# A streaming encoder block on one core: the pool inputs' gates moved to slots 3 and 5 of the next pair, the output pair's forms made in three steps over two slots

## The chip, the core and the metric

The kernel runs on one core of a Trainium2 chip. Four engines do the work: PE multiplies matrices (its weight loads are shown apart as PEld), DVE does element-wise work on two operands, ACT does casts, copies and activation functions, POOL is nearly idle; SP issues transfers. Each engine works its own list of instructions in program order, and semaphores make one wait for another. The metric is the device time of one execution in microseconds (us). Three runs of the kernel before gave 1829.51, 1828.97 and 1829.35 us: median 1829.35.

## What is computed

One encoder block for 256 tokens of width 4096, in fp32. A mixer sub-layer projects the normalised tokens by one wide matrix and splits the result; one part feeds attention, another a multi-scale pooling whose output is gated. Both go through an output projection and onto the residual; a cross-attention sub-layer follows. The lines that the change concerns:

```python
q, k, v, gate_a, u_b, gate_b = jnp.split(h @ w_in, ...)
y_a = att * jax.nn.silu(gate_a)
y_b = multiscale_pool(u_b, w_pool, pool_scale) * jax.nn.silu(gate_b)   # 4 groups of 512 channels
y = jnp.concatenate([y_a, y_b], axis=-1) @ w_out
x = x + rmsnorm(y, g_post)
# multiscale_pool: trailing mean over 2, 4, 8 or 16 tokens, minus the token; then a 512 x 512 map; then a scale
# silu(g) = g * sigmoid(g) = 0.5 * g * (tanh(g / 2) + 1)
```

## The kernel before

**Weights as a stream.** All weights come as 648 chunks of 128 x 1024 ("subs"). PE works one sub per *slot*; the loop at line 1264 runs over slots. A fp32 product is made of three matmuls on rounded parts: a value is split into `wh`, its rounded value (ACT, line 201), and `wl`, what rounding left (DVE, line 202), and PE adds high x high, low x high and high x low (lines 324 to 326). A sub is split two or three slots ahead of the slot that uses it; there are four raw buffers and five pairs `wh`/`wl`, so the split engines can run ahead of PE by a few slots and no more.

**Pairs.** The first 520 subs are worked in 16 *pairs* of output strips: A and B for attention, then U 0 to 3 (the pool inputs with their gates), then O 0 to 3 (the output projection). A pair takes 32 slots; U 1 to 3 and O 0 take 34, since the two pool subs (512 x 512 map) of the U pair before stand in them. Most pairs save products on some of their 16 *quads* (two slots each) by working on sums of blocks: those quads are "fast" and need four splits, two of them of sums in `tt` (functions `quad_sums`, `quad_split`, `quad_rest`). O 0 is worked directly, without fast quads.

**After a pair.** With e the slot behind a U pair's last one, the results `c11`, `c21` (first strip: the pool input) and `c12`, `c22` (second strip: the gate input, in `e_u`) are finished on DVE in slots e and e + 1 (`late1`, `late2`). In slot e + 2 PE turns the pool input (`pool_u`). DVE makes trailing sums (`pool_sum`, line 730) and the differences (`pool_d`, lines 738 to 741) for two halves, which ACT rounds (line 743) and DVE finishes (line 747). `gate` turns a gate input g into g (1 + tanh(g/2)): a tanh on ACT (line 510), then one instruction on DVE (line 511). PE then turns each gate (`pool_turn`, line 500) in slots e + 9 and e + 12, in the middle of its stream of matmuls: if the gate is not ready, PE stands.

**Forms of the output pair.** The outputs of attention and pool lie in DRAM (`yd`). For each of 16 chunks c of 256 rows, `load_y` fetches chunk c, and `y_forms` makes the parts that PE multiplies in O 0: ACT rounds the chunk, DVE subtracts (lines 253, 254); for the even chunks from 2 on (`FAST["out"]`) DVE also makes four sums of its blocks in `tt` (lines 401 to 404), and ACT and DVE split those as well. All of it stands in one slot i, three slots ahead of the chunk's first use.

**Order.** Nothing reorders the lists. Within a slot come the entries of `first_at`, then the splits of weights, then the entries of `at`, then the slot's matmuls:

```python
for i in range(-3, n + TAIL + 1):
    for f, a in firsts.pop(i, []): f(*a)
    for f, a in jobs.pop(i, []): f(*a)
    for f, a in tasks.pop(i, []): f(*a)
    if 0 <= i < n + TAIL: mm(i)
```

U 0 ends at slot 288, U 1 at 322, U 2 at 356, U 3 at 390. So the last gate's turn stands in slots 300, 334, 368 and 402.

Of the kernel before, what the change touches and what calls it, by code (L numbers as in the profile page):

```python
# [10 lines left out]
F32 = mybir.dt.float32  # L11
# [5 lines left out]
P = 128  # L17
# [27 lines left out]
FAST = {"in": (2, 4, 7, 9, 12, 14), "out": (2, 4, 6, 8, 10, 12, 14)}  # L45
# [8 lines left out]
def fast_quads(pair):  # L54
    if pair in DIRECT:
        return ()
    f = FAST[stage_of(pair)]
    return tuple(c for c in f if c > 7) if pair == ("B", 0) else f
# [67 lines left out]
def block_kernel(ctx: ExitStack, tc: tile.TileContext, x, mem, ws, relb, vecs, out):  # L126
# [26 lines left out]
    def buf(tag, shape, name, dtype=F32, bufs=1):  # L153
        return com.tile(shape, dtype, tag=tag, name=name, bufs=bufs)
# [3 lines left out]
    def at(i, f, *a):  # L158
        tasks.setdefault(i, []).append((f, a))

    def first_at(i, f, *a):

        firsts.setdefault(i, []).append((f, a))
# [4 lines left out]
    def tiles(ap):  # L168
        return ap.rearrange("p (a b) -> p a b", b=P)
# [4 lines left out]
    V, A, T_ = nc.vector, nc.scalar, nc.tensor  # L174


    tt = buf("T", [P, 1536], "tt")
# [57 lines left out]
    for s in range(n):  # L235
# [6 lines left out]
        else:  # L242
            i = s - (2 if wide and m[1] > fast_quads(m[0])[0] else 3)
# [7 lines left out]
    def split_copy(h, l, src):  # L251

        A.copy(h, src)
        V.tensor_sub(l, src, h.bitcast(F32))
# [99 lines left out]
    def end(*key):  # L354
        return max(where[key].values())
# [24 lines left out]
    def block(stage, c):  # L380

        tag, o, u = HOME[stage, c]
        f = forms[tag][:, 256 * o:256 * (o + u)]
        return tiles(f[:, :u * P]), tiles(f[:, u * P:])
# [14 lines left out]
    def sums_of(a11, a21, a12, a22, dst):  # L399

        V.tensor_add(dst[:, 1, :], a21, a22)
        V.tensor_sub(dst[:, 2, :], dst[:, 1, :], a11)
        V.tensor_sub(dst[:, 3, :], a11, a21)
        V.tensor_sub(dst[:, 0, :], a12, dst[:, 2, :])
# [108 lines left out]
    for pair in PAIRS:  # L513
        if pair not in DIRECT:
            at(slot[pair, fast_quads(pair)[-1], 1] + 1, early, pair)
        e = end_slot[pair]
# [58 lines left out]
    for c in range(QUADS):  # L575
        i = first + (3 * c) // 2
# [112 lines left out]
    for hg in range(4):  # L689
        e = end_slot["A", hg]  # L690
# [4 lines left out]
        e = end_slot["B", hg]  # L695
        at(e + 2, b_turn, hg, 0)
        at(e + 3, b_turn, hg, 1)
        for j in range(4):
            h, o = 4 * hg + j, e + 6 + 7 * j
# [60 lines left out]
    for g in range(4):  # L760
        e = end_slot["U", g]
        at(e + 2, pool_u, g)
        for b in range(2):
            i = e + 3 + 4 * b
            for j in range(g + 1):
                at(i + j // 2, pool_sum, g, b, j)
            at(i + 2, pool_d, g, b)
            at(i + 3, pool_rest, g, b)
            at(e + 6 + 4 * b, gate, ("U", g), ("c12", "c22")[b])
            at(e + 9 + 3 * b, pool_turn, g, b)  # L770
            j = end("pool", g, 2 * b)
            first_at(j + 2, pool_y, g, 2 * b)
            for c in range(2):
                at(j + 3 + c, y_store, 16 + 4 * g + 2 * b + c, "sg", 2 * b + c)


    ych = {}
# [4 lines left out]
        ych[c] = hd["yin", c % 4 // 2][:, c % 2, :, :]  # L782
        nc.sync.dma_start(ych[c], yd[c])

    def y_forms(c):
        src = ych.pop(c)
        u = src.rearrange("p a (t b) -> p (a t) b", b=P)
        h, l = block("out", c)
        split_copy(h[:, 0:4, :], l[:, 0:4, :], u)
        if c in FAST["out"]:  # L790
            s = tiles(tt[:, 0:512])
            sums_of(u[:, 0, :], u[:, 1, :], u[:, 2, :], u[:, 3, :], s)
            split_copy(h[:, 4:8, :], l[:, 4:8, :], s)

    for c in range(QUADS):
        i = slot[("O", 0), c, 0] - 3
        at(i - (4 if c < QUADS - 2 else 3), load_y, c)
        at(i, y_forms, c)


    x2t = []
# [16 lines left out]
    for m in range(4):  # L818
        e = end_slot["O", m]
# [120 lines left out]
    b = e_out + 10  # L940
    room = begin("xq", 0) - b - 1
    for c in range(KT // 2):
        i = b + (c * room) // (KT // 2)
# [79 lines left out]
    e = end("xq", 7)  # L1023
    for h in range(XH):
        i = end("xq", 2 * h + 1)
# [4 lines left out]
    for h in (0, 1):  # L1030
        i = end("xq", 2 * h + 1)
# [8 lines left out]
    e = end("xv", 1)  # L1040
# [23 lines left out]
    for c in range(first_tail):  # L1064
        e = end("xo", c) + 1
# [91 lines left out]
    v, g = nc.vector, nc.gpsimd  # L1157
    s_, o_ = tail_scale, tail_out
    at(n - TAIL + 3, tail_base)
    for t in range(2):  # L1160
        e = n - TAIL // 2 + TAIL * t
# [5 lines left out]
    e = n  # L1167
# [13 lines left out]
    e = n + TAIL  # L1181
# [82 lines left out]
    for i in range(-3, n + TAIL + 1):  # L1264
        s = i + 3
# [92 lines left out]
```

## Time and profile before

| | |
|---|---|
| median of three runs | 1829.35 us |
| the profiled execution's own time | 1829.09 us |
| its span in the trace, first to last instruction | 1827.2 us |
| PE busy | 1801.1 us (99%) |
| DVE busy | 1487.7 us (81%) |
| ACT busy | 1053.2 us (58%) |
| mean granted TensorE clock | 0.995 |

The span is 1.9 us shorter than the execution's own time; the difference is what lies around the first and the last instruction. PE's busy share hides two things: a matmul's end is modelled, so that one of 0.39 us is followed by the next after 0.23 us, and a matmul at half the clock counts as busy as well. What PE loses is read from its waits and from the starts of its matmuls.

### The profile page before, as it was taken

The numbers are of one execution on the slowest core, as the hardware profiler recorded it, in microseconds if no ns is written. First come the engines' busy times: TensorE is split into PE (matmuls) and PEld (weight loads), VectorE is DVE, ScalarE is ACT, GpSimd is POOL, SyncE is SP. The second block draws the span as 40 slices with busy tenths as digits, with TensorE's granted clock in tenths as the row PEclk, the third lists the DMA queues.
The fourth block names the chain that finished last, engine by engine and source line by source line (L and its number), as shares of the span: only waits on it lengthen the run. The fifth ranks groups of instructions, "written<-read, shape, count | busy, mean of one in ns | idle before, by whom it ended". The sixth has DMA issues, their size and how long they took to land.

```text
span 1827.2 us, 23882 instructions
## 1 busy us (share of the span) xinstructions
PE 1801.1 (99%) x8459; PEld 1502.9 (82%) x8459; DVE 1487.7 (81%) x1969; ACT 1053.2 (58%) x1435; POOL 17.3 (1%) x20
## 2 busy tenths in 40 slices
PE   9999999999999999999999998999999999999997
PEld 8888888888888888888888787888888888888885
DVE  8884788878888888888888887688889899656686
ACT  8564565565655655655555554555555677545553
POOL 0000000000000000000000000000000000000002
PEclk9999999999999999999999999999999999999998
DMA  8775565656556565556555575656556777556654
GB/s 314 256 241 193 172 209 190 208 184 211 199 200 203 188 210 189 206 184 215 191 201 201 190 245 201 217 185 207 190 198 206 249 254 262 187 171 221 205 192 131
DMA packets 122903, 378.13 MB, mean 207 GB/s; under 512 B 12960, under 2 KB 27424, under 8 KB 122784
## 3 DMA queue, kind: packets, MB, share of 16 engines
q1 hardware_dynamic: 121056, 375.56, 60.4%
q8 instruction: 66, 1.08, 0.2%
q10 hardware_dynamic: 1728, 1.05, 0.2%
q14 instruction: 53, 0.43, 0.1%
HBM read 368.17 MB, written 8.39 MB: 206 GB/s over the span
## 4 chain that ended last, share of the span: by engine, by line
PE 88%; DVE 6%; issue 3%; ACT 2%; DMA 1%; POOL 0%; DVEq 0%; ACTq 0%; POOLq 0%
PE P L324 16%; PE P L325 16%; PE P L326 16%; PE acc L319 6%; PE c L324 5%; PE c L325 5%; PE c L326 5%; DVE wl L202 3%; PE acc L320 3%; PE xk L324 2%; PE xv L326 2%; PE xk L326 2%; PE xv L324 2%; PE xv L325 2%; PE xk L325 2%
## 5 line engine op out<-in xcount | busy, mean ns | idle before, releaser
L202 DVE TENSOR_TENSOR wl<-raw,wh 128x1024 fp32r<-128x1024 f32 (+1 forms) x646 | 780.4, 1220 | 201.3 <-ACT wh L201 189.1
L201 ACT CAST wh<-raw 128x1024 fp32r<-128x1024 f32 (+1 forms) x646 | 672.8, 1049 | 347.2 <-DMA raw<-ws_dram 100.9
L324 PE MATMUL P<-wh,Fa 128*128 128x512 f32 x917 | 359.6, 392 | 0.0
L326 PE MATMUL P<-wl,Fa 128*128 128x512 f32 x917 | 357.3, 390 | 0.0
L325 PE MATMUL P<-wh,Fa 128*128 128x512 f32 x917 | 357.0, 389 | 0.0
L324 PE MATMUL P<-wh,Fb 128*128 128x512 f32 x612 | 241.4, 394 | 0.0
L326 PE MATMUL P<-wl,Fb 128*128 128x512 f32 x612 | 238.8, 390 | 1.5 <-DVE wl L202 1.5
L325 PE MATMUL P<-wh,Fb 128*128 128x512 f32 x612 | 238.3, 389 | 0.0
L201 ACT CAST wh<-tt 128x1024 fp32r<-128x1024 f32 (+1 forms) x162 | 128.1, 834 | 143.6 <-DVE tt L225 126.7
L326 PEld LDWEIGHTS P<-wl,Fa 128*128 128x128 f32 x917 | 172.1, 188 | 37.2 <-DVE wl L202 1.0
L325 PEld LDWEIGHTS P<-wh,Fa 128*128 128x128 f32 x917 | 172.3, 188 | 34.4
L324 PEld LDWEIGHTS P<-wh,Fa 128*128 128x128 f32 x917 | 172.2, 188 | 34.3
L202 DVE TENSOR_TENSOR wl<-tt,wh 128x1024 fp32r<-128x1024 f32 (+1 forms) x162 | 148.3, 955 | 37.6 <-ACT wh L201 35.7
L326 PEld LDWEIGHTS P<-wl,Fb 128*128 128x128 f32 x612 | 114.8, 188 | 27.0 <-DVE wl L202 2.8
L325 PEld LDWEIGHTS P<-wh,Fb 128*128 128x128 f32 x612 | 115.0, 188 | 22.7
L324 PEld LDWEIGHTS P<-wh,Fb 128*128 128x128 f32 x612 | 114.9, 188 | 22.4
L324 PE MATMUL c<-wh,Fa 128*128 128x512 f32 x268 | 106.1, 396 | 0.0
L326 PE MATMUL c<-wl,Fa 128*128 128x512 f32 x268 | 105.4, 393 | 0.0
L325 PE MATMUL c<-wh,Fa 128*128 128x512 f32 x268 | 105.2, 393 | 0.0
L319 PE MATMUL acc<-h2HL,wh 128*128 128x512 f32 x256 | 91.4, 400 | 0.0
L216 DVE TENSOR_TENSOR tt<-raw 128x512 f32<-128x512 f32 x81 | 55.7, 688 | 25.4 <-DMA raw<-ws_dram 24.8
L320 PE MATMUL acc<-h2HL,wl 128*128 128x256 f32 x256 | 71.8, 280 | 0.0
(297 smaller groups left out, 2417.6 us busy)
## 6 DMA issues: line engine op xcount, KB each, us to landing
raw<-ws_dram SPq DMA_DIRECT2D x647, 512.0 KB, 4.1
tt<-x_dram SPq DMA_DIRECT2D x31, 256.0 KB, 4.3
lc<-mem_dram SPq DMA_DIRECT2D x24, 256.0 KB, 4.0
yd<-sg SPq DMA_DIRECT2D x32, 128.0 KB, 4.8
yin<-yd SPq DMA_DIRECT2D x16, 256.0 KB, 4.7
lc<-x_dram SPq DMA_DIRECT2D x16, 256.0 KB, 4.1
out_dram<-y SPq DMA_DIRECT2D x13, 256.0 KB, 2.8
x<-relb_dram SPq DMA_DIRECT2D x16, 192.0 KB, 5.0
```

The source lines that it names most:

```text
L201: A.copy(h[:, c], src[:, c])
L202: V.tensor_sub(l[:, c], src[:, c], h[:, c].bitcast(F32))
L216: V.tensor_sub(tt[:, 0:512], r2[:, 512:], r1[:, 512:])
L319: T_.matmul(acc, H[:, w], X, start=first, stop=last, skip_group_check=True)
L320: T_.matmul(acc[:, :S], L[:, w], X[:, :S], start=False, stop=last, skip_group_check=True)
L324: T_.matmul(acc, xs[0], w[0], start=first, stop=False)
L325: T_.matmul(acc, xs[1], w[0], start=False, stop=False)
L326: T_.matmul(acc, xs[0], w[1], start=False, stop=last)
```

## The change

The gates of the U pairs are asked for in slots e + 3 and e + 5 in place of e + 6 and e + 10. The turns stay in slots e + 9 and e + 12. The forms of a chunk, which stood in slot i, are made in three steps: the sums at the head of slot i - 1, the rounding at the head of slot i, the subtraction at its end. The sums now go to two halves of `tt` in turn. The gates of the A pairs (`a_gates`) and all transfers stay in their slots.

```diff
-            at(e + 6 + 4 * b, gate, ("U", g), ("c12", "c22")[b])
+            at(e + 3 + 2 * b, gate, ("U", g), ("c12", "c22")[b])
...
-    def y_forms(c):
-        src = ych.pop(c)
-        u = src.rearrange("p a (t b) -> p (a t) b", b=P)
+    def y_sums(c):
+        u = ych[c].rearrange("p a (t b) -> p (a t) b", b=P)
+        ych[c] = [u]
+        if c in FAST["out"]:
+            t = tiles(tt[:, 512 * (c // 2 % 2):512 * (c // 2 % 2) + 512])
+            sums_of(u[:, 0, :], u[:, 1, :], u[:, 2, :], u[:, 3, :], t)
+            ych[c].append(t)
+
+    def y_round(c):
+        for j, t in enumerate(ych[c]):
+            A.copy(block("out", c)[0][:, 4 * j:4 * j + 4, :], t)
+
+    def y_rest(c):
         h, l = block("out", c)
-        split_copy(h[:, 0:4, :], l[:, 0:4, :], u)
-        if c in FAST["out"]:
-            s = tiles(tt[:, 0:512])
-            sums_of(u[:, 0, :], u[:, 1, :], u[:, 2, :], u[:, 3, :], s)
-            split_copy(h[:, 4:8, :], l[:, 4:8, :], s)
+        for j, t in enumerate(ych.pop(c)):
+            V.tensor_sub(l[:, 4 * j:4 * j + 4, :], t, h[:, 4 * j:4 * j + 4, :].bitcast(F32))
...
-        at(i, y_forms, c)
+        first_at(i - 1, y_sums, c)
+        first_at(i, y_round, c)
+        at(i, y_rest, c)
```

In these pieces the lines of the changed kernel are its own: its lines 795 and 800 stand for 253 and 254 of the kernel before. `e_u_73` is the gate input of the first token half (`c12`), `e_u_74` that of the second (`c22`); `ahl` and `d_6844` take the two halves of the pool differences.

DVE's list behind U 2, slots 361 to 363, as one piece of the difference:

```order
 L740 SCALAR_TENSOR_TENSOR w<-w,u 128x2x256
 L741 TENSOR_TENSOR w<-f,u 128x2x16
+L511 SCALAR_TENSOR_TENSOR e_u_74<-x_80,e_u_74 128x512
 L202 TENSOR_TENSOR wl<-raw,wh 128x1024 x2
 L225 TENSOR_TENSOR tt<-raw 128x512
 L226 TENSOR_TENSOR tt<-raw,tt 128x512
 L747 TENSOR_TENSOR ahl<-w,ahl 128x2x256
-L511 SCALAR_TENSOR_TENSOR e_u_73<-x_80,e_u_73 128x512
 L202 TENSOR_TENSOR wl<-tt,wh 128x1024
```

The second gate's instruction now stands ahead of the splits of the fast quad in slots 364 and 365, and the first gate's has left the place behind them (it stands three slots earlier).

DVE's list behind U 3, slots 399 to 402, in the kernel before:

```order
L741 TENSOR_TENSOR w<-f,u 128x2x16
L254 TENSOR_TENSOR Fa_76<-yin,Fa_76 128x512
L401 TENSOR_TENSOR tt<-yin 128x128
L402 TENSOR_TENSOR tt<-tt,yin 128x128
L403 TENSOR_TENSOR tt<-yin 128x128
L404 TENSOR_TENSOR tt<-yin,tt 128x128
L254 TENSOR_TENSOR Fa_76<-tt,Fa_76 128x512
L202 TENSOR_TENSOR wl<-raw,wh 128x1024
L747 TENSOR_TENSOR d_6844<-w,d_6844 128x2x256
L511 SCALAR_TENSOR_TENSOR e_u_74<-x_80,e_u_74 128x512
L202 TENSOR_TENSOR wl<-raw,wh 128x1024 x2
```

The same slots in the changed kernel:

```order
L741 TENSOR_TENSOR w<-f,u 128x2x16
L800 TENSOR_TENSOR Fa_76<-yin,Fa_76 128x512
L800 TENSOR_TENSOR Fa_76<-tt,Fa_76 128x512
L202 TENSOR_TENSOR wl<-raw,wh 128x1024
L747 TENSOR_TENSOR d_6844<-w,d_6844 128x2x256
L202 TENSOR_TENSOR wl<-raw,wh 128x1024 x2
```

The four sums of chunk 6 and the second gate's instruction have left these slots; the split of sub 403 (the first L202) and the rest of the pool difference follow sooner.

ACT's list at the same place, kernel before:

```order
L504 ACTIVATE sg<-tn 128x4x128
L743 CAST d_6844<-w 128x2x256
L253 CAST Fa_76<-yin 128x512
L253 CAST Fa_76<-tt 128x512
L201 CAST wh<-raw 128x1024
L510 ACTIVATE x_80<-e_u_74 128x512
L201 CAST wh<-raw 128x1024 x2
```

And in the changed kernel:

```order
L795 CAST Fa_76<-yin 128x512
L795 CAST Fa_76<-tt 128x512
L201 CAST wh<-raw 128x1024
L504 ACTIVATE sg<-tn 128x4x128
L743 CAST d_6844<-w 128x2x256
L201 CAST wh<-raw 128x1024 x2
```

The two roundings of chunk 6 have moved ahead of the cast L743, which waits for DVE, and the tanh is gone from between the casts of weights.

## Rows read from the trace of the kernel before

**Rows 1.** The page, part 1: busy time, share of span, instructions.

```profile
PE 1801.1 (99%) x8459; PEld 1502.9 (82%) x8459; DVE 1487.7 (81%) x1969; ACT 1053.2 (58%) x1435; POOL 17.3 (1%) x20
```

**Rows 2.** Waits of PE: total us, times, longest us.

```profile
PE tn L500 <- DVE e_u L511: 9.1, 4, 5.5
...
PE P L326 <- DVE wl L202: 1.5, 2, 0.7
```

**Rows 3.** Timeline of PE: start, us, what [idle before, and its releaser].

```profile
834.85 0.66 PE L500 MATMUL tn<-ident,e_u 128*128 128x128 f32 x4 [0.97 <-DVE e_u L511]
...
1021.63 0.66 PE L500 MATMUL tn<-ident,e_u 128*128 128x128 f32 x4 [1.58 <-DVE e_u L511]
...
1105.05 0.60 PE L500 MATMUL tn<-ident,e_u 128*128 128x128 f32 x4
1105.41 0.48 PE L324 MATMUL c<-wh,Fb 128*128 128x512 f32 x1
...
1108.24 0.39 PE L324 MATMUL c<-wh,Fb 128*128 128x512 f32 x1
...
1113.46 0.39 PE L326 MATMUL c<-wl,Fb 128*128 128x512 f32 x1
1119.39 1.11 PE L500 MATMUL tn<-ident,e_u 128*128 128x128 f32 x4 [5.55 <-DVE e_u L511]
1120.16 0.77 PE L324 MATMUL c<-wh,Fa 128*128 128x512 f32 x1
...
1125.42 0.43 PE L324 MATMUL c<-wh,Fa 128*128 128x512 f32 x1
```

**Rows 4.** Stretches by engine: PE, PEld, DVE, ACT, POOL busy, then PEclk, DMA.

```profile
1119.40:1125.40 6.00, 6.00 (x16) 4.85 (x17) 4.13 (x4) 2.17 (x4) 0.00 (x0) 0.50 0.87 300
```

**Rows 5.** Timeline of DVE behind U 2, slots 360 to 368.

```profile
998.64 1.23 DVE L202 TENSOR_TENSOR wl<-raw,wh 128x1024 fp32r<-128x1024 f32 x1 [1.10 <-ACT wh L201]
...
1005.62 2.36 DVE L202 TENSOR_TENSOR wl<-raw,wh 128x1024 fp32r<-128x1024 f32 x2 [1.64 <-ACT wh L201]
...
1019.15 1.23 DVE L202 TENSOR_TENSOR wl<-raw,wh 128x1024 fp32r<-128x1024 f32 x1 [1.64 <-ACT wh L201]
```

**Rows 6.** Timeline of ACT behind U 2 (tanh) and U 3 (rounding of pool differences).

```profile
1006.45 0.62 ACT L510 ACTIVATE x<-e_u 128x512 f32<-128x512 f32 x1
...
1112.48 0.62 ACT L743 CAST d<-w 128x512 fp32r<-128x512 f32 x1 [5.84 <-DVE w L741]
```

**Rows 7.** Timeline of DVE behind U 3, slots 391 to 400.

```profile
1087.14 0.69 DVE L254 TENSOR_TENSOR Fb<-tt,Fb 128x512 fp32r<-128x512 f32 x1 [0.69 <-ACT Fb L253]
...
1090.01 1.23 DVE L202 TENSOR_TENSOR wl<-raw,wh 128x1024 fp32r<-128x1024 f32 x1 [0.69 <-ACT wh L201]
...
1097.63 0.20 DVE L741 TENSOR_TENSOR w<-f,u 128x32 f32<-128x32 f32 x1
1099.03 0.69 DVE L254 TENSOR_TENSOR Fb<-yin,Fb 128x512 fp32r<-128x512 f32 x1 [1.21 <-ACT Fb L253]
...
1100.37 0.28 DVE L404 TENSOR_TENSOR tt<-yin,tt 128x128 f32<-128x128 f32 x1
...
1102.30 1.23 DVE L202 TENSOR_TENSOR wl<-raw,wh 128x1024 fp32r<-128x1024 f32 x1 [0.27 <-ACT wh L201]
...
1112.26 0.19 DVE L741 TENSOR_TENSOR w<-f,u 128x32 f32<-128x32 f32 x1
...
1116.91 1.23 DVE L202 TENSOR_TENSOR wl<-raw,wh 128x1024 fp32r<-128x1024 f32 x1 [0.25 <-ACT wh L201]
1118.05 0.69 DVE L747 TENSOR_TENSOR d<-w,d 128x512 fp32r<-128x512 f32 x1
1118.65 0.68 DVE L511 SCALAR_TENSOR_TENSOR e_u<-x,e_u 128x512 f32<-128x512 f32 x1
```

**Rows 8.** The line of `load_y` (L783), and its issue for chunk 2 on SP.

```profile
DMA to landing us min/median/max: 3.6/4.7/6.5
...
1074.90 0.42 SPq L783 DMA_DIRECT2D yin<-yd x1
```

## The prediction

> **What bounds the kernel now.** I read the page's busy times first, then the waits of PE, then PE's timeline around those waits, and last the lists of DVE and ACT just before them. The page shows PE busy for 99% of the span [rows 1], so only what PE loses counts. The waits name one large loser: four turns of a gate (L500) wait for the gate's instruction on DVE (L511), 9.1 us in all, against 1.5 us for a weight split [rows 2]. The timeline gives their places: 0.97 us at 834.85 behind U 0, 1.58 us behind U 2, 5.55 us behind U 3 [rows 3]; what is left of the 9.1 is 0.97 us, behind U 1. All four are the second gate's turn, slot e + 12.
>
> These idle times understate the loss in two ways. A matmul shown with 0.39 us is followed by the next after (1108.24 - 1105.41) / 12 = 0.24 us, so that each gap costs 0.15 us more than its idle time. And behind the long gap PE is slow: the turn takes 0.77 us to the next matmul where it took 0.36, and the twelve matmuls of slot 402 take 1125.42 - 1120.16 = 5.26 us where those of slot 399 took 2.83 [rows 3]. The granted clock says why: 0.50 in that stretch, the lower of the two levels, 1.2 GHz [rows 4].
>
> Why is the gate late behind U 3? PE had taken slot 401 at 1113.46, while DVE was still in slot 400: the split of sub 403 began at 1116.91 and the gate at 1118.65 [rows 7]. DVE was two slots late, because it and ACT waited for each other: DVE 1.21 us for the rounding of a chunk that stood on ACT behind L743, and ACT 5.84 us for the difference that L743 rounds [rows 6, 7].
>
> **What goes.** Where the gates' instructions finish before the turns, PE gets back:
> - behind U 0 and U 1: 0.97 + 0.15 = 1.12 us each, 2.24;
> - behind U 2: 1.58 + 0.15 = 1.73;
> - behind U 3: 1119.39 - 1113.46 - 0.24 = 5.69, then 0.77 - 0.36 = 0.41 for the turn and 5.26 - 2.83 = 2.43 for the twelve matmuls.
>
> The sum is 12.5 us. For its clock part, 2.84 us, I take the rows. The Trainium skill (TensorE: Matmul & The Clock Gate, section Terms) would have it as the throttled time times one minus the clock's share, an estimate of 6.0 x 0.5 = 3.0 us [rows 4] and a sum of 12.7; the rows differ from it by 0.2, and they decide.
>
> **What moves, behind U 0 to U 2.** No instruction is added: eight tanh and eight gate instructions change places. The first gate (slot e + 3) falls into a gap: behind U 2, DVE waited 1.10 us for a cast before 998.64 [rows 5], and the instruction needs 0.60 (start to start, 1118.05 to 1118.65 [rows 7]). The second gate (slot e + 5) is worse placed. Its tanh stands on ACT behind L743 and ahead of the casts of the next fast quad, and DVE's list stands behind it; the split at 1005.62, which waited 1.64 us for that ACT chain [rows 5], comes later by the tanh, 0.62 us [rows 6] less some 0.09 of overlap: 0.53. But the first gate's instruction has left the place behind these splits, which gives 0.60 back before the quad's second half. Net I take 0, from -0.07 to +0.53 at each of three boundaries, since the two halves are in one list and nothing but DVE's own sums waits between them. The two waits for a split, 1.5 us together [rows 2], I leave as they are. Late next, once the turn behind U 2 starts at 1021.63 - 1.73 = 1019.90, is the split of that slot's own sub, which ends at 1019.15 + 1.23 = 1020.38 [rows 5]; the third matmul after the turn, the first to read it, would come about 0.9 us after the turn's start, at 1020.8. That is 0.4 us to spare; behind U 0 and U 1 PE gains less, so more is left.
>
> **What moves, behind U 3.** Here the lists must be followed, since both edits meet. The instructions per chunk are the same: two casts, two subtractions and four sums for a fast one. The four sums take (1100.37 + 0.28) - (1099.03 + 0.60) = 1.02 us [rows 7].
> - *Slots 390 to 393.* With the sums of chunk 2 a slot early, the waits of 0.69 us at 1087.14 and at 1090.01 have no cause [rows 7]. The split at 1090.01 comes at 1088.63.
> - *To the first difference (L741).* Before, 1097.63 - 1090.01 = 7.62 us. Now the first gate (0.60) and the sums of chunk 4 (1.02) stand in between: 1088.63 + 9.24 = 1097.87. So far nothing is won, but more work is done.
> - *To slot 396.* Before, DVE waited 1.21 us for ACT's L743 and a rounding; now for L743 and the second tanh, as long: gate at 1099.3. Then the gate and two subtractions, 3 x 0.60: the split that began at 1102.30 begins at 1101.1.
> - *To the second difference.* Before, 1112.26 - 1102.30 = 9.96 us. The first gate has left (-0.60), the sums of chunk 6 have come in (+1.02): 1101.1 + 10.38 = 1111.5.
> - *Split of sub 403.* ACT's list now has only L743 and that cast, some 1.6 us, behind the difference; the split begins at 1113.3 instead of 1116.91 and ends at 1114.5, and the pool difference is ready at 1115.1.
>
> PE, without the wait, turns the gate at 1113.70, begins slot 402 at 1114.06 and slot 403 at 1116.89, and first reads the split of 403 with its third matmul, at 1117.36: 2.9 us to spare. The pool sub of slot 404 follows at 1119.7, with its inputs there at 1116.3. So no wait takes the old one's place, and without a long gap I see nothing that would lower the clock.
>
> One thing is new: the sums read a chunk one slot sooner than its rounding did, and the loads do not move. Loads of these chunks took 3.6 to 6.5 us to land, 4.7 in the median [rows 8]. Chunk 2's left at 1074.90, so that it lands between 1078.5 and 1081.4. The whole spread, 2.9 us, is what is spare at slot 403: at the worst PE begins to wait there, for nothing to 0.5 us. After slot 404 no turn stands in PE's stream, and DVE is as far ahead as the buffers allow.
>
> **The sum.** 12.5 us off the profiled execution's 1829.09 is 1816.6; the median of the runs lies 0.26 us above that execution, so the forecast is 1829.35 - 12.5 = 1816.85 us, 0.7% less. Its own range is 1816 to 1818.
>
> **Rivals.**
> 1. *DVE stays late behind U 3 and a split or pool wait takes the turn's place.* Speaking for it: DVE's list is as long as before, 81% busy overall [rows 1], and my walk wins only where it waited for ACT. If it wins nothing there, the split of 403 ends at 1118.14 against a need at 1117.36, which costs 0.8; a landing at 6.5 instead of 4.7 adds 1.8. Such gaps are smaller than the one that the lower clock followed. 1829.35 - 12.5 + 0.8 to 2.6 = 1817.65 to 1819.45.
> 2. *The second gate's place costs what it gains behind U 0 to U 2.* DVE has no lead there, as the two waits for splits show [rows 2]; if the 0.53 us is not paid back, and the 0.4 us to spare is gone too, the boundaries give up to 4.0 us less: 1818.4 to 1820.8. Against it: the instruction that leaves is as long as the one that comes.
> 3. *The turns wait for something else than L511*, and the change does nothing: 1829.35. Against it: the turns begin 0.06 us after L511 ends (1118.65 + 0.68 = 1119.33, PE at 1119.39 [rows 3, 7]).
> 4. *Slower.* The second tanh stands on ACT behind L743, and DVE's list stands with it. If it waited there as long as L743 itself did, 5.84 us [rows 6], then every boundary would have PE stand as it stood behind U 3, 5.69 + 0.41 + 2.43 = 8.5 us with the clock's part: four times that against 12.5 now, 1816.85 + 34.1 = 1851. It decides against the change from 12.5 / 4 = 3.1 us a boundary. Against it: L743's wait is ended by L741, which stands directly before the gate in DVE's own list, so that only L743 and the tanh remain to be waited for, 1.2 us.
>
> **Chances.** Forecast 0.72, first rival 0.13, second 0.08, third 0.03, fourth 0.04. A difference of less than 0.2% (3.7 us) cannot be told from none here; the forecast and the first two rivals are all faster by more: 0.93 faster, 0.03 the same, 0.04 slower. The range runs from 1815.4 (the splits' waits of 1.5 us gone as well) to 1820.4, which holds the forecast, the first rival and nearly all of the second.
>
> **What would show it.** In the profile after: no wait of L500 for L511; the granted clock at 1.00 from 1100 to 1140 us; waits of L326 for a split still about 1.5 us; the gates' instructions behind U 3 within some 7 us of each other, and the split of sub 403 begun about 3.6 us sooner, relative to PE's slot 401, than before. I am wrong if PE has a new gap of over 1 us between slots 390 and 410, if the quads behind U 0 to U 2 show waits for splits of more than 0.7 us each, or if the lower clock still appears in the middle of the run.

## The result, and the profile after

The changed kernel takes 1817.28 us in the median of four runs (1817.18 to 1817.58), the kernel before 1829.31 us beside it (1828.97 to 1829.51). The ratio is 0.9934, with a 95% interval of 0.9921 to 0.9946: 12.0 us less, where 12.5 were forecast. The profiled execution of the changed kernel took 1817.58 us, its span 1815.8 us, at a mean granted clock of 0.997.

First the busy line of its page, against [rows 1].

```profile
PE 1797.2 (99%) x8459; PEld 1501.3 (83%) x8459; DVE 1485.6 (82%) x1969; ACT 1052.3 (58%) x1435; POOL 17.3 (1%) x20
```

No engine has lost or gained an instruction; PE shows 4 us less and still 99%. What was won was idle time and half-rate time, which shares don't tell. The waits of PE do (total us, times, longest us), against [rows 2]:

```profile
PE mr L1118 <- DVE tt L1114: 2.2, 1, 2.2
PE P L326 <- DVE wl L202: 1.5, 2, 0.7
PE warm L1271 <- DVE half L1267: 1.1, 1, 1.1
PE pt L660 <- ACT wh L201: 1.0, 4, 0.3
PE c L326 <- DVE wl L202: 0.5, 1, 0.5
PE P L324 <- DVE e_t L478: 0.4, 1, 0.4
```

The line of 9.1 us, L500 for L511, is gone. The 1.5 us for splits stand as they stood. Two small lines belong to the start of the program (below).

PE's timeline gives the places, against [rows 3]: the turns behind U 0, U 1, U 2, both turns behind U 3, and slots 402 and 403 behind the last one.

```profile
835.31 0.60 PE L500 MATMUL tn<-ident,e_u 128*128 128x128 f32 x4
...
926.97 0.60 PE L500 MATMUL tn<-ident,e_u 128*128 128x128 f32 x4
...
1018.97 0.60 PE L500 MATMUL tn<-ident,e_u 128*128 128x128 f32 x4
...
1102.29 0.60 PE L500 MATMUL tn<-ident,e_u 128*128 128x128 f32 x4
...
1110.71 0.39 PE L326 MATMUL c<-wl,Fb 128*128 128x512 f32 x1
1110.94 0.60 PE L500 MATMUL tn<-ident,e_u 128*128 128x128 f32 x4
1111.29 0.48 PE L324 MATMUL c<-wh,Fa 128*128 128x512 f32 x1
...
1114.12 0.39 PE L324 MATMUL c<-wh,Fa 128*128 128x512 f32 x1
```

No turn has an idle time before it. Behind U 3 the turn takes 0.35 us to the next matmul and slot 402 takes 1114.12 - 1111.29 = 2.83 us, as other slots do; before, these were 0.77 and 5.26. The granted clock around that place, against [rows 4] (columns as there), stays at 2.4 GHz, the upper of the two levels:

```profile
1107.90:1113.80 5.90, 5.90 (x30) 4.90 (x29) 5.43 (x8) 5.12 (x7) 0.00 (x0) 1.00 0.58 178
1113.80:1119.40 5.60, 5.60 (x37) 5.05 (x36) 4.05 (x8) 3.27 (x5) 0.00 (x0) 1.00 0.78 286
```

What each place gave is read from matmuls of the same number in the two traces. The shift is a matmul's start in the changed kernel less its start before, so that a minus sign means sooner. The gain of a place is the shift of the matmul directly ahead of the turn less the shift of the turn (at U 3, of the first matmul of slot 403).

| place | shift ahead of it, us | shift behind it, us | gain | forecast |
|---|---|---|---|---|
| U 0 | +1.60 | +0.47 | 1.13 | 1.12 |
| U 1 | +0.37 | -0.75 | 1.12 | 1.12 |
| U 2 | -0.93 | -2.66 | 1.73 | 1.73 |
| U 3, to slot 403 | -2.75 | -11.31 | 8.56 | 8.53 |
| sum | | | 12.54 | 12.50 |

The last row, for one, is 1125.42 - 1114.12 = 11.30 against 1105.05 - 1102.29 = 2.76 at the first turn [rows 3]. The table begins at +1.60: ahead of U 0 the profiled execution lost 1.0 us in its first 10.3 us (c L326, 0.5 us idle, stands there) and 0.6 at 451 us (P L324, 0.4 us idle). Nothing of the change stands there.

Behind U 3, DVE's list in the changed kernel (start, us, what), against [rows 7]:

```profile
1088.27 0.68 DVE L511 SCALAR_TENSOR_TENSOR e_u<-x,e_u 128x512 f32<-128x512 f32 x1
...
1094.95 0.19 DVE L741 TENSOR_TENSOR w<-f,u 128x32 f32<-128x32 f32 x1
1096.36 0.69 DVE L511 SCALAR_TENSOR_TENSOR e_u<-x,e_u 128x512 f32<-128x512 f32 x1 [1.22 <-ACT x L510]
...
1098.17 1.22 DVE L202 TENSOR_TENSOR wl<-raw,wh 128x1024 fp32r<-128x1024 f32 x1
...
1108.46 0.19 DVE L741 TENSOR_TENSOR w<-f,u 128x32 f32<-128x32 f32 x1
1108.57 0.68 DVE L800 TENSOR_TENSOR Fa<-yin,Fa 128x512 fp32r<-128x512 f32 x1
...
1110.29 1.23 DVE L202 TENSOR_TENSOR wl<-raw,wh 128x1024 fp32r<-128x1024 f32 x1 [0.44 <-ACT wh L201]
1111.43 0.68 DVE L747 TENSOR_TENSOR d<-w,d 128x512 fp32r<-128x512 f32 x1
...
1116.00 0.29 DVE L401 TENSOR_TENSOR tt<-yin 128x128 f32<-128x128 f32 x1 [1.01 <-DMA yin<-yd]
```

and ACT's at the same place, against [rows 6]:

```profile
1095.17 0.62 ACT L743 CAST ahl<-w 128x512 fp32r<-128x512 f32 x1 [3.07 <-DVE w L741]
1095.70 0.63 ACT L510 ACTIVATE x<-e_u 128x512 f32<-128x512 f32 x1
...
1108.68 0.62 ACT L743 CAST d<-w 128x512 fp32r<-128x512 f32 x1 [2.59 <-DVE w L741]
1109.21 2.00 ACT L201 CAST wh<-raw 128x1024 fp32r<-128x1024 f32 x2
```

Two things are to be seen. Behind the second difference (1108.46) DVE subtracts at once, where it waited 1.21 us before:

```profile
1113.66 0.69 DVE L254 TENSOR_TENSOR Fa<-yin,Fa 128x512 fp32r<-128x512 f32 x1 [1.21 <-ACT Fa L253]
```

And the split of sub 403 begins at 1110.29, 0.65 us ahead of PE's turn; before, it began 3.21 us behind PE's arrival (1116.91 - 0.24 - 1113.46). The second thing is that behind the first difference DVE still waits: 1.22 us, now for the tanh, which stands behind L743.

### The profile page after: what moved, and what is told of

Read it like the earlier page. It is cut to its first block, busy times and chain, and to the rows that moved or that the text cites. A ratio compares the mean times of both kernels' runs of the same rounds, so it can differ in the third digit from the quotient of the medians.

```text
span 1815.8 us, 23862 instructions
## 1 busy us (share of the span) xinstructions
PE 1797.2 (99%) x8459; PEld 1501.3 (83%) x8459; DVE 1485.6 (82%) x1969; ACT 1052.3 (58%) x1435; POOL 17.3 (1%) x20
## 3 DMA queue, kind: packets, MB, share of 16 engines
q10 hardware_dynamic: 1728, 1.05, 0.2%
## 4 chain that ended last, share of the span: by engine, by line
PE 90%; DVE 5%; issue 2%; ACT 2%; DMA 1%; POOL 0%; SPq 0%; DVEq 0%; ACTq 0%; POOLq 0%
PE P L326 17%; PE P L324 17%; PE P L325 17%; PE acc L319 6%; PE c L326 5%; PE c L324 5%; PE c L325 5%; PE acc L320 3%; DVE wl L202 2%; PE xk L324 2%; PE xv L324 2%; PE xk L325 2%; PE xv L325 2%; PE xv L326 2%; PE xk L326 2%
## 5 line engine op out<-in xcount | busy, mean ns | idle before, releaser
L202 DVE TENSOR_TENSOR wl<-raw,wh 128x1024 fp32r<-128x1024 f32 (+1 forms) x646 | 779.9, 1220 | 186.0 <-ACT wh L201 174.4
L324 PE MATMUL P<-wh,Fa 128*128 128x512 f32 x917 | 359.8, 392 | 0.0
L326 PE MATMUL P<-wl,Fa 128*128 128x512 f32 x917 | 357.6, 390 | 0.1
L324 PE MATMUL P<-wh,Fb 128*128 128x512 f32 x612 | 241.7, 395 | 0.4 <-DVE e_t L478 0.4
L326 PE MATMUL P<-wl,Fb 128*128 128x512 f32 x612 | 239.0, 391 | 1.5 <-DVE wl L202 1.5
L326 PEld LDWEIGHTS P<-wl,Fa 128*128 128x128 f32 x917 | 172.2, 188 | 37.4 <-DVE wl L202 1.2
L324 PEld LDWEIGHTS P<-wh,Fa 128*128 128x128 f32 x917 | 172.3, 188 | 34.2
L202 DVE TENSOR_TENSOR wl<-tt,wh 128x1024 fp32r<-128x1024 f32 (+1 forms) x162 | 148.1, 954 | 37.4 <-ACT wh L201 35.2
L326 PEld LDWEIGHTS P<-wl,Fb 128*128 128x128 f32 x612 | 114.9, 188 | 26.9 <-DVE wl L202 2.7
L324 PEld LDWEIGHTS P<-wh,Fb 128*128 128x128 f32 x612 | 115.0, 188 | 23.1 <-DVE e_t L478 0.8
L324 PE MATMUL c<-wh,Fa 128*128 128x512 f32 x268 | 105.1, 392 | 0.2 <-ACT wh L201 0.2
L326 PE MATMUL c<-wl,Fa 128*128 128x512 f32 x268 | 104.6, 390 | 0.5 <-DVE wl L202 0.5
```

What stands on the lines that cost most here:

```text
L202: V.tensor_sub(l[:, c], src[:, c], h[:, c].bitcast(F32))
L324: T_.matmul(acc, xs[0], w[0], start=first, stop=False)
L326: T_.matmul(acc, xs[0], w[1], start=False, stop=last)
```

## The experiments

Two theories stood. *Late DVE*: the turns waited because DVE and ACT, waiting for each other, ran late, and the lower clock came of the long gap that this made on PE. *The rivals*: one of the two edits does all, or does harm that the other covers; the lower clock has another cause; the second gate's new place costs something. The kernel before, beside each set of kernels, gave 1828.41 (1827.39 to 1829.37, 14 runs; e1, e2, e3 and the first late cast) and 1828.58 (1827.62 to 1829.32, 9 runs; the others).

**The gates alone.** The kernel before, with one line changed:

```diff
-            at(e + 6 + 4 * b, gate, ("U", g), ("c12", "c22")[b])
+            at(e + 3 + 2 * b, gate, ("U", g), ("c12", "c22")[b])
```

> The kernel before with the gates in slots e+3 and e+5, the forms of the output pair as before. My theory (both edits matter behind U 3, the gates alone behind U 0 to U 2): the four waits of a turn for the gate go; behind U 3 DVE and ACT still wait for each other, now with the second gate's instruction ahead of the split of sub 403, which then ends 0.6 us later than before (1118.7 in the time of the trace before) against a need at 1117.36: a wait of L326 for a split of about 1.4 us in slot 403, clock 1.00. About 1818.7 us, 10.6 us under before. Rival A (the forms play no part): 1817.3 as the changed kernel, no wait in slots 399 to 405. Rival B (without the forms PE still has a gap long enough for the lower clock): 1824 or more, granted clock 0.50 behind U 3.

Measured: 1818.80 us (1817.45 to 1820.37), ratio 0.995 (0.9933 to 0.9966). U 0 to U 2 give 1.13, 1.12 and 1.73 us by the same shifts; from the first turn behind U 3 to the fourth matmul of slot 403 it gives 7.0 us instead of 8.56. One wait of about 1.4 us was expected in slot 403; there are two, 0.75 us of idle time. PE's timeline shows where the rest went, behind the last turn:

```profile
1110.35 0.50 PE L325 MATMUL c<-wh,Fa 128*128 128x512 f32 x1 [0.23 <-DVE Fa L254]
...
1114.15 0.50 PE L326 MATMUL c<-wl,Fa 128*128 128x512 f32 x1 [0.52 <-DVE wl L202]
```

and DVE's why: it waits for ACT's roundings, and the split of sub 403 begins 3.67 us behind the last turn (1112.87 against 1109.20 in this trace), where the changed kernel has it 0.65 us ahead.

```profile
1109.61 0.69 DVE L254 TENSOR_TENSOR Fa<-yin,Fa 128x512 fp32r<-128x512 f32 x1 [1.21 <-ACT Fa L253]
...
1111.91 0.69 DVE L254 TENSOR_TENSOR Fa<-tt,Fa 128x512 fp32r<-128x512 f32 x1 [0.69 <-ACT Fa L253]
1112.87 1.23 DVE L202 TENSOR_TENSOR wl<-raw,wh 128x1024 fp32r<-128x1024 f32 x1 [0.26 <-ACT wh L201]
```

So the gates give most of it, and the forms in steps some 1.5 us more by the places.

**The forms alone.** The changed kernel with the gates' line put back.

> The changed kernel with the gates back in slots e+6 and e+10, the forms in three steps. My theory: behind U 0, U 1, U 2 the turns wait for L511 as before (1.0, 1.0, 1.6 us idle, 4.0 us lost with the matmul spacing); behind U 3 DVE is some 5 us sooner than before, so that the last turn waits about 0.6 us instead of 5.55 and the clock stays at 1.00. About 1821.9 us, 7.4 under before: the two gains overlap by some 6 us behind U 3. Rival A (the gate's place is what matters, the forms do nothing by themselves): 1829, a gap of over 5 us and clock 0.50 behind U 3. Rival B (forms help, but a gap of 2 to 4 us stays): 1823 to 1825.

Measured: 1822.50 us (1821.54 to 1823.04), ratio 0.9966 (0.9953 to 0.9979). The waits of PE, and the last turn:

```profile
PE tn L500 <- DVE e_u L511: 4.6, 4, 1.6
```

```profile
1114.60 0.66 PE L500 MATMUL tn<-ident,e_u 128*128 128x128 f32 x4 [1.14 <-DVE e_u L511]
```

The four waits stay; the last is 1.14 us instead of 5.55 (0.6 was expected), and the mean clock is 0.997. Either edit alone brings PE's shift behind U 3 to some 7 us (7.17 here, from -0.39 to -7.56), both bring 8.56. The two gains overlap, because each alone shortens the long gap to under 1.2 us, and the 2.84 us of the lower clock go with the gap, once. Which of the three steps does it (the earlier sums, the earlier rounding or the second half of `tt`) was not tested apart.

**The clock by itself.** The kernel before, and in slot 402, ahead of its last turn, 20 small products on ones that nothing reads (40 matmuls in the trace). They add work and take no wait away.

```diff
+    def fill():
+        w = bank("fill")
+        for _ in range(20):
+            T_.matmul(w[:, :P], ones, ones, start=True, stop=True)
+        done(w)
...
+            if g == 3 and b == 1:
+                at(e + 12, fill)
```

> The kernel before with 20 extra matmuls of ones (128x128, two passes each, some 4.6 us at the higher level) in slot 402 ahead of the last turn, into a free bank: the wait for the gate stays, but PE works through most of it. My theory (the half-rate stretch behind U 3 comes of PE's idle time there): the turn still starts when L511 ends, the granted clock stays at 1.00 and 2.84 us come back: 1826.5 us. Rival A (the slow matmuls behind the gap have another cause, such as the transfers that run at 0.87 share there): 1829.3, the twelve matmuls of slot 402 still take 5.3 us. Rival B (the extra matmuls run past the gate's time and cost as much as they save): 1828 to 1830 with the clock at 1.00.

Measured: 1826.46 us (1826.05 to 1827.32, ten runs), ratio 0.9989 (0.998 to 0.9998). PE's timeline, and the stretch that stood at 0.50 before [rows 4]:

```profile
1113.85 4.63 PE L755 MATMUL fill<-ones 128*128 128x128 f32 x40
1119.26 0.63 PE L500 MATMUL tn<-ident,e_u 128*128 128x128 f32 x4 [0.78 <-DVE e_u L511]
1119.64 0.47 PE L324 MATMUL c<-wh,Fa 128*128 128x512 f32 x1
...
1122.49 0.39 PE L324 MATMUL c<-wh,Fa 128*128 128x512 f32 x1
```

```profile
1119.40:1125.40 6.00, 6.00 (x30) 5.02 (x30) 5.62 (x7) 3.63 (x5) 0.00 (x0) 1.00 0.95 328
```

The turn comes as late as before, at 1119.26, since the gate is as late; but PE was busy in between, the clock stays at 1.00, and slot 402 takes 1122.49 - 1119.64 = 2.85 us. The turn takes 0.38 to the next matmul. Against 5.26 and 0.77 that is 2.80 us, the 2.84 us of the forecast within 0.04. So the half-rate stretch followed from PE's idleness and not from the place or the data; nor from the transfers, whose share is 0.95 in this stretch at the clock of 1.00, and was 0.87 at 0.50 [rows 4]. The medians differ by 1.95 us, in runs that spread over 2 us.

**The second gate's place.** The changed kernel with the first gate put behind the second (slots e + 6 and e + 5 instead of e + 3 and e + 5). Then nothing leaves the place behind the next quad's splits to make up for what the second gate puts in front of them.

```diff
-            at(e + 3 + 2 * b, gate, ("U", g), ("c12", "c22")[b])
+            at(e + 6 - b, gate, ("U", g), ("c12", "c22")[b])
```

> The changed kernel with only the second gate moved (slot e+5), the first back in slot e+6. My theory (behind U 0 to U 2 the second gate's 0.5 us ahead of the fast quad is paid back only because the first gate leaves the place behind it): the second half of the quad is split 0.6 us later, waits of L326 for a split rise from 1.5 to about 3 us, and each of the three boundaries loses 0.5 to 0.6: 1.7 us over the changed kernel of the same comparison. Rival (DVE has room for the first gate in either place): no difference to the changed kernel, waits of L326 still 1.5 us.

The changed kernel was run again beside it:

> The changed kernel once more, beside the next three on one chip. Its first four runs lay at 1817.28 us, 12.0 under the kernel before, while the places in its trace give 12.5 and its start gave 1.7 us back that no edit touches. My theory (the start varies from run to run): 11 to 13.5 us under the kernel before of this comparison, a start of the first 450 us that is up to 2 us later or not later at all from one execution to another. Rival (the change makes the start slower): the 1.7 us stand in the profile again.

Measured: 1818.03 us (1817.58 to 1818.39) against 1816.82 (1815.69 to 1817.86) for the changed kernel: 1.2 us more in the median, where the ranges of the runs touch. By the shifts from ahead of U 0 to slot 403 behind U 3 it gains 10.99 us (+0.20 to -10.79) where the repeat gains 12.98 (-0.29 to -13.27): 2.0 us less. The direction was right, the place was not. The waits for splits did not grow; the *first* turn, in slot e + 9, waits for its gate. PE's waits, and that turn behind U 2:

```profile
PE P L326 <- DVE wl L202: 1.4, 2, 0.7
PE tn L500 <- DVE e_u L511: 1.3, 3, 0.6
```

```profile
1010.16 0.63 PE L500 MATMUL tn<-ident,e_u 128*128 128x128 f32 x4 [0.57 <-DVE e_u L511]
```

DVE's list at that place shows the first gate and the split behind it:

```profile
1009.33 0.68 DVE L511 SCALAR_TENSOR_TENSOR e_u<-x,e_u 128x512 f32<-128x512 f32 x1
1009.93 1.82 DVE L202 TENSOR_TENSOR wl<-tt,wh 128x1024 fp32r<-128x1024 f32 x2
```

The three idle times are 0.51, 0.19 and 0.57 us, 1.27 together; with the 0.15 us that each costs beyond its idle time that is 1.72, most of the 2.0. The expected 1.7 us thus came by another path than the one named; that the size agrees is luck. The split behind the gate begins 0.23 us ahead of the turn, against 0.11 in the repeat of the changed kernel (1007.53, its turn at 1007.64): because PE had waited for the gate, the split is no later for PE than it was. I had priced the later of two readers, and the earlier one set the loss. The first gate moved alone was not run.

The repeat of the changed kernel has a ratio of 0.9935 (0.9923 to 0.9948), and in its trace the four places give 1.14, 1.13, 1.73 and 8.56 us, 12.56, from a start shifted by -0.35 instead of +1.60. The places repeat to 0.01 us; what lies ahead of U 0 does not.

**The cast one slot later.** The remaining waits for a split (1.5 us) stand behind the wait of 1.22 us on DVE, which comes of ACT: L743 holds the tanh and the casts of weights while it waits for the difference. So L743 was put into a step of its own, one slot later, and L747 behind it.

```diff
         V.tensor_sub(d[:, :, 0:16], f, u[:, :, 16:32])
-        hl = pg["d"][b]
-        A.copy(hl[:, :, :S], d)
+
+    def pool_cast(g, b):
+        o = 2 * (g % 2)
+        A.copy(pg["d"][b][:, :, :S], pg["w"][:, o:o + 2, 16:])
...
-            at(i + 3, pool_rest, g, b)
+            at(i + 3, pool_cast, g, b)
+            at(i + 4, pool_rest, g, b)
```

> The changed kernel with the rounding of the pool differences (L743) one slot later, behind that slot's casts of weights, and its subtraction (L747) one slot later still. My theory (behind U 1 and U 2 the two remaining waits for a split, 0.73 us idle and 0.88 us lost each, come of ACT's casts standing behind L743 while L743 waits for DVE): DVE's waits of 1.2 to 1.6 us for a cast behind each difference go, and both waits of L326 with them: about 1815.3 us, 2.0 under the changed kernel. Rival (DVE's own work is too long there, the waits stay whatever the order): 1817.3, waits of L326 still 1.5 us.

> The changed kernel with the late rounding once more, on one chip with the changed kernel. By the places in the two traces it is 2.0 us under it, by the medians of two comparisons on different chips 3.5. My theory: 2.0 us, the rest came of the chips and the start. Rival: 3.5 us.

Measured: 1813.78 us (1813.46 to 1815.17), ratio 0.9921 (0.9906 to 0.9935), and again 1813.56 (1813.40 to 1813.96), ratio 0.9918 (0.9904 to 0.9931). Of the second run, DVE's list behind U 2:

```profile
1000.40 0.68 DVE L511 SCALAR_TENSOR_TENSOR e_u<-x,e_u 128x512 f32<-128x512 f32 x1
1001.00 2.35 DVE L202 TENSOR_TENSOR wl<-raw,wh 128x1024 fp32r<-128x1024 f32 x2
...
1005.13 1.83 DVE L202 TENSOR_TENSOR wl<-tt,wh 128x1024 fp32r<-128x1024 f32 x2 [0.45 <-ACT wh L201]
```

and the same in the repeat of the changed kernel:

```profile
1002.38 0.69 DVE L511 SCALAR_TENSOR_TENSOR e_u<-x,e_u 128x512 f32<-128x512 f32 x1 [1.22 <-ACT x L510]
1003.32 2.36 DVE L202 TENSOR_TENSOR wl<-raw,wh 128x1024 fp32r<-128x1024 f32 x2 [0.25 <-ACT wh L201]
...
1007.53 1.82 DVE L202 TENSOR_TENSOR wl<-tt,wh 128x1024 fp32r<-128x1024 f32 x2
```

The waits of 1.22 and 0.25 us are gone, and one of 0.45 has come in. Gone with them are PE's waits for a split behind U 1 and, but for 0.10 us, behind U 2. Behind U 0 no such wait was listed, but four matmuls began 0.33 to 0.44 us behind the ones before them in the changed kernel, and none of these over 0.24 in the late cast. Since these waits stand between a pair's two turns, the places are counted here from the first turn: in both traces of the late cast U 0 gives 1.66 to 1.67 us, U 1 2.22, U 2 2.58 to 2.61 and U 3 8.57, 15.05 in all; the change gives 12.4 counted so, 2.65 less. The medians of the runs beside each other are 3.26 us apart (1816.82 and 1813.56). Both are more than the 2.0 that I had expected; the expectation priced only the two listed waits. The 0.6 us between shifts and medians are not settled; they lie within the spread of the changed kernel's own runs.

**The late cast without the forms in steps.** The kernel before, with the gates' new slots and the late cast.

> The kernel before with the gates in slots e+3 and e+5 and the rounding of the pool differences one slot later, but the forms of the output pair in one step as before. My theory (what DVE and ACT lose behind U 3 to the forms is about as much as they lose to L743, and either edit brings DVE ahead of PE there): no wait in slots 399 to 405, the two waits of L326 gone: within 0.5 us of the kernel with both edits and the late rounding, so 2.0 us under the changed kernel. Rival (the forms in three steps are needed behind U 3): the 1.4 us of the kernel with the gates alone stay in slots 402 and 403: 0.6 us under the changed kernel.

Measured: 1814.18 us (1813.37 to 1814.56), ratio 0.992 (0.9907 to 0.9934). By the places, counted from the first turn, it gives 1.66, 2.22, 2.62 and 8.56 us, the same as with the forms in steps. DVE waits 0.69 us for a rounding as in the kernel before, and then makes the split of sub 403:

```profile
1108.19 0.69 DVE L254 TENSOR_TENSOR Fa<-tt,Fa 128x512 fp32r<-128x512 f32 x1 [0.69 <-ACT Fa L253]
1109.14 1.23 DVE L202 TENSOR_TENSOR wl<-raw,wh 128x1024 fp32r<-128x1024 f32 x1 [0.26 <-ACT wh L201]
```

PE has its last turn at 1107.38 here and the third matmul of slot 403 at 1111.02; the split ends at 1110.37, 0.65 us ahead of its reader, where the changed kernel has 3.05 (1114.57 against 1111.52). That is enough: what the forms in steps add with the late cast is spare time that PE does not use. The lowest median is that of the changed kernel with the late cast; the two late-cast kernels differ by 0.4 to 0.6 us in the median, which is not a proven difference.

## Why the prediction was right

**The terms.** Each of the four places gave its term to 0.03 us (table above). The reading behind them holds: a turn's wait costs its idle time and 0.15 us, and the long gap costs the turn and the twelve matmuls of slot 402 at half the clock; the run with the filled gap shows this price by itself, 2.80 us where 2.84 were reckoned.

**What was taken as nothing at U 0 to U 2.** The waits for splits stayed at 1.5 us in two, as said. The net of nothing is seen behind U 2: PE gains 0.22 us ahead of the first turn (shift -0.83 to -1.05) and loses 0.12 behind it (to -0.93). There the spare time named as next, 0.4 us, is 0.44 (the split begun at 1018.21 ends at 1019.43, the third matmul begins at 1019.87). The first gate's new place is what pays: with the second gate moved alone, 1.27 us come back as idle time at the first turns.

**The walk behind U 3.** It was reckoned in the time of the kernel before, in which PE stood 2.75 us later: first difference at 1097.87 (measured 1094.95 + 2.75 = 1097.70), gate at 1099.3 (1099.11), split at 1101.1 (1100.92), second difference at 1111.5 (1111.21), split of sub 403 at 1113.3 (1113.04). The split was to begin 3.6 us sooner against PE and began 3.21 + 0.65 = 3.86 sooner; it was to have 2.9 us to spare and has 3.05.

**The first rival**, DVE late behind U 3, is what the gates alone show: a wait for a form and one for a split take 1.5 us, within the 0.8 to 2.6 named. The forms in steps take it away. **The second rival** appears only where the first gate doesn't leave. **The third and the fourth** fall: no turn waits, and the wait of 1.22 us behind L743 was L743 and the tanh alone (1.2 forecast), not 5.84.

**The signs.** The granted clock is 1.00 from 1100 to 1140 us. Two signs came out otherwise: the gates' instructions behind U 3 stand 8.1 us apart (1088.27 and 1096.36) and not within some 7; and the two waits for splits, 0.73 and 0.72 us, lie above the 0.7 named as a sign of being wrong. They are those of the kernel before, at the same two matmuls (0.73 each), so that they do not come of the change.

**What was off.** The forecast was 0.43 us low, and the places are not to blame: they gave 12.54. The profiled execution had lost 1.6 us ahead of U 0, the repeat none; but the repeat's median too is only 11.8 us under the kernel before, so that one execution's start does not account for it, and it stays open where the medians lose 0.5 to 0.8 us against the places. The loads that DVE waits for were looked for at the wrong chunk: not chunk 2's (0.22 us) but the later ones, chunk 8's (1.01 us at 1116.00) and others up to 2.31 us, five waits of 6.0 us in all where the kernel before had none. I had passed over them with "as far ahead as the buffers allow"; they cost nothing here, since PE has no wait there and its shift stays at -11.4 us. And the splits' remaining 1.5 us were left as they are, at U 1 and U 2; the cause, a cast that waits at the head of ACT's list, stood in rows I had read [rows 5, 6], and one slot of delay takes them away but for 0.10 us.

## What to carry to other kernels

Where two engines work lists in order and wait for each other, an instruction that waits long (here a cast for a difference) holds everything behind it; to put it later, or to put what is ready ahead of it, can be worth more than to shorten anything. Price a gap on the matmul engine by the starts of its matmuls, which show more than its idle time, and by the clock behind it, and don't add the gains of two edits that end the same gap. Where a place moves to make room, look first at the earliest reader behind it, which may be a step of another kind than the one you fear.

## What the runs showed of the hardware

Between 20 and 1795 us the lower clock came behind a gap of 5.55 us on PE, and not behind the turns' gaps of 0.19 to 1.58 us: from 20 to 1110 us and from 1130 to 1795 us the mean granted clock is 1.00 in every trace; the stretches around the last turn stay at 1.00 in the changed kernel and in the filled one, and slot 402 keeps its usual pace with the forms alone, behind a gap of 1.14 us (1117.64 - 1115.33 = 2.31 us from its second to its last matmul, where the kernel before took 1125.00 - 1120.73 = 4.27). Ahead of U 0 two executions of one and the same kernel differ by up to 2 us (+1.60 and -0.35 for the changed one), by short waits that come and go, so that a difference of 1 us is read from shifts at the place and not from one execution's total.
